# Three gathers in fp32 and a router without GpSimd in a mixture-of-experts layer

## The chip, the cores and the metric

The kernel runs on one core of one Trainium2 chip. Its time is the device time of one execution, in microseconds (us). Before the change it was 1368.84 us, the median of three runs (1368.73, 1368.84, 1371.41).

## The reference, cut to what matters

One transformer-like layer: a token mixer (two recurrent branches), then a mixture-of-experts block of 32 experts with the best four for each of 256 tokens. The change touches the passage from the mixer to the experts and the first visits of the experts.

```python
x = x + g1[:, None, :] * rmsnorm(yl, norm_mix_post[l])
hl = modulate(rmsnorm(x, norm_ffn_pre[l]), sh2, sc2)
# moe_ffn(hl, ...):
logits = xf.astype(f32) @ w_router + b_router
top_v, top_e = lax.top_k(logits, TOP_K)            # 4 of 32
wts = jax.nn.softmax(top_v, axis=-1)
...                                                # tokens sorted by expert, xblk: tokens of expert e
gate, up = jnp.split(xblk @ w_gu[e] + b_gu[e], 2, axis=-1)
gate = jnp.minimum(gate, 7.0); up = jnp.clip(up, -7.0, 7.0)
act = (up + 1) * gate * jax.nn.sigmoid(1.702 * gate)
y = act @ w_dn[e] + b_dn[e]                        # weighted, summed per token
```

D_MODEL and the experts' width are 1024; w_gu of an expert is 1024 x 2048 fp32 (8 MB), w_dn 1024 x 1024 fp32 (4 MB). All 32 experts are read in every run, 403 MB in all.

## The kernel before, in words

**Visits.** The 256 tokens lie as two chunks of 128 on the partitions. Behind the mixer come 33 visits: one for each expert in the list `turn`, and one extra for the fullest expert. A visit serves up to 64 tokens. It gathers them (a product of the normed tokens with a 0/1 matrix `oh`, so the tokens come out transposed, and `modulated` on ScalarE applies scale and shift, L1382), multiplies them with w_gu (`products`, L1600: eight groups k of rows, in the two PSUM banks pg and pu), applies the gate (`gated`, L1610 to L1616), transposes the result (`act_T`, L1629 to L1631), multiplies with w_dn (`down`, L1650), takes the result in two parts (`two_parts`, L1641 and L1642), and adds it to the tokens it came from (`scatter`, L1660, with VectorE's weighted sum into `acc`, which is the space `h2`). The bias goes first into pg and pu (`bias`, L1338).

**Order in a visit.** A visit n begins with the bias, `act_T` of the visit before, the down products of the visit before, then its own gate and up products with the two scatters of the visit before between them, then `gated`. The first two visits have no result to scatter yet; the first visit's down products and scatter stand at the end of visit n = 1.

**Weights.** They come in chunks of 2 MB through a ring of nine buffers. SyncE's queue issues the loads in order; each waits until TensorE has used up the chunk that was in its buffer. Exceptions are the first expert's chunks: its fourth is two halves of 1 MB, one in `scr_`, one in the second half of the tile `xr`, which is `h2`. Then follow the second expert's w_dn, the third's w_gu (four loads) and w_dn (two), the fourth's w_gu, and so on.

**A gather in three parts.** The normed tokens are kept as three bf16 parts, hb0, hb1, hb2, whose sum has fp32's precision: hb0 = bf16(x1 r2), hb1 = bf16(x1 r2 - hb0), hb2 = the rest. A gather is 3 parts x 2 chunks x 8 blocks = 48 products of 128x128 weights with 64 columns of bf16 (L1572; L1376 for the first gather).

**The passage before the visits.** Everything from L1386 on is under a written-out order (`manual_schedule`): each engine runs its instructions in the order of the code. For each chunk: `residual` (VectorE), `squares` (ScalarE), the norm r2 (`second_norm` and its end), transposes (`turned`), logits on TensorE, `logits_back`, `select` (VectorE: best four, 0/1 matrix mbf), the ranks of the tokens within their expert (products with mbf into `rk`), `token_slots` (VectorE: R and the first expert's oh0). Beside it the parts are made: `part(0)` and `part(1)` on ScalarE, `rest` (the remainder, kept in fp32 in h2) on GpSimd for chunk 0 and VectorE for chunk 1, `part(2)` on GpSimd, the last one on VectorE (L1359). Then `first_tokens` (TensorE) for each chunk, `modulated`, and the first visit.

Of the kernel before, what the change touches and what calls it, by code (L numbers as in the profile page):

```python
# [17 lines left out]
P = 128  # L18
# [46 lines left out]
def layer_kernel(ctx: ExitStack, tc, x, ctxt, w_ada, b_ada, n_mix_post, n_ffn_post, w_in, b_in, w_pa, w_pb, w_out,  # L65
# [1038 lines left out]
    for i, u in enumerate(units[1:], 1):  # L1104
        ada_runs[:] = [0] if (i, 0) in rest_at or (i, 1) in rest_at else []
        if u[2]:
            u[2]()
        cur, nxt = nxt, prep(units[i + 1] if i + 1 < len(units) else (lambda: mraw[0],))
        for j, blk in enumerate(u[1](*cur)):
            blk()  # L1110
            for _ in range(rest_at.get((i, j), 0)):
                next(rest)
            if len(convs) > 2 or i > 0 and convs:
                with after(mods[-1:]):
                    convs.pop(0)()
            step(2 if work and len(work) <= 2 or i > 11 else 1)
            for f, *args in load_at.get((i, j), ()):
                if not gu_first:
                    step(100)
                    M["stack"].close()  # L1120
                    vps.close()
                    fps.close()
                    wr1 = pool("wr1", stack=moe)
                    rl = pool("rl", stack=moe)
                    hb0, hb2 = (rl.tile([P, 2, D], BF, name=n) for n in ("hb0", "hb2"))
# [164 lines left out]
    oh0 = hmh[:, 1024:1088].bitcast(BF).rearrange("p (c s) -> p c s", c=2)  # L1290
    hb = [hb0, hb1, hb2]
    big = hmh[:, 1152:1216].rearrange("p (c e) -> p c e", c=2)
    lgs = [None, None]
# [16 lines left out]
    def logits_back(ch, lT):  # L1310
# [2 lines left out]
        lgs[ch] = psm.tile([P, 4, E], F32, name="lgs", tag="tr", bufs=1)  # L1313
        nc.tensor.transpose(lgs[ch].rearrange("p k e -> p (k e)"), l_sb, ident)

    def select(ch):

        nc.vector.tensor_reduce(lsum[:, ch], lgs[ch].rearrange("p k e -> p e k"), AX.X, OP.add)
# [9 lines left out]
    def bias(u, e, n=CAP, sel=None):  # L1328
# [5 lines left out]
        bank = p_.tile([P, 512], F32, name=t, tag=t, bufs=1 + (t == "sc"))[:, 0:W]  # L1334
        sel = pk if sel is None else sel
        for g in range(G):
            j, c0 = divmod(D * u + W * g, 512)
            nc.tensor.matmul(bank[n * g:n * g + n, :], sel[:, 4 * e + j:4 * e + j + 1].to_broadcast([P, n]),  # L1338
                             bgu[:, c0:c0 + W], start=True, stop=False, skip_group_check=True)
        return bank  # L1340

    def biases(*args, **kw):
        return [bias(u, *args, **kw) for u in range(2)]

    def token_slots(ch):

        nc.vector.tensor_scalar(big[:, ch], mbf[:, ch], -BIG, BIG, op0=OP.mult, op1=OP.add)
        nc.vector.tensor_add(R[:, ch], rk[:, ch], big[:, ch])
        nc.vector.tensor_scalar(oh0[:, ch], iot, R[:, ch, turn[0]:turn[0] + 1], None, op0=OP.is_equal)
# [6 lines left out]
    def part(i, ch, hf, eng=nc.scalar):  # L1356
        d, h, x_, r2 = blocks4(hb[i], ch, hf), paired(h2, ch, hf), paired(x1, ch, hf), yss[:, 2 + ch:3 + ch]
        if i == 2:
            eng.tensor_tensor(d, h, blocks4(hb1, ch, hf), op=OP.subtract)  # L1359
        elif i == 1:  # L1360
            nc.scalar.copy(d, h)
        else:
            nc.scalar.activation(d, x_, AF.Identity, scale=r2)

    def rest(ch, hf, eng):
        h, x_, r2, h0 = paired(h2, ch, hf), paired(x1, ch, hf), yss[:, 2 + ch:3 + ch], blocks4(hb0, ch, hf)
        if eng is nc.vector:
            eng.scalar_tensor_tensor(h, x_, r2, h0, op0=OP.mult, op1=OP.subtract)
        else:
            eng.tensor_scalar(h, x_, r2, None, op0=OP.mult)  # L1370
            eng.tensor_tensor(h, h, h0, op=OP.subtract)

    def first_tokens(ch):
        for i in range(3):
            for k in range(KB):
                nc.tensor.matmul(xp[:, k], hb[i][:, ch, k * P:(k + 1) * P], oh0[:, ch],  # L1376
                                 start=(ch == 0 and i == 0 and k == 0), stop=(ch == 1 and i == 2), skip_group_check=True)
# [5 lines left out]

    t00, t01 = turned(0, 0), turned(0, 1)
    end2()
    end1 = leave(1, 1, lambda: first_norm(1))  # L1386
    pmm_.close()
    pb = pool("pb", PSUM, moe)
    nc.scalar.copy(xT[0][0], t00)
    nc.scalar.copy(xT[0][1], t01)  # L1390
    part(0, 0, 0)
    rest(0, 0, nc.gpsimd)
    lT = logits(0)
    end1()
# [22 lines left out]
    part(0, 1, 0)
    part(0, 1, 1)
    part(1, 0, 1)
    part(2, 0, 0, nc.gpsimd)  # L1420
# [12 lines left out]
    oh1 = hmh[:, 1088:1152].bitcast(BF).rearrange("p (c s) -> p c s", c=2)
    for ch in range(2):
        nc.vector.tensor_scalar(oh1[:, ch], iot, R[:, ch, turn[1]:turn[1] + 1], None, op0=OP.is_equal)
    first_tokens(1)
# [293 lines left out]
    visits.insert(HV + 1, (EH, E))  # L1730
    NV = len(visits)
    prev = None
    xgs, ohs, ohTs = {0: xg}, {1: oh1}, {0: ohT}
    for n, (e, col) in enumerate(visits):
        final = n == NV - 1
        if n >= 2 and col < E:
# [24 lines left out]
        if n + 2 < NV and n < 2:  # L1761
            ohs[n + 2] = selection(visits[n + 2][1])
        if n > 1:
            products(banks, gu, xgs[n], range(0, 2))
            scatter(pcol, ohTs[n - 1], 0)
            if n + 2 < NV:
                ohs[n + 2] = selection(visits[n + 2][1])
            products(banks, gu, xgs[n], range(2, 3))
            scatter(pcol, ohTs[n - 1], 1)
            if n < NV - 1:  # L1770
                ohTs[n + 1] = slots(ohs[n + 1])
            products(banks, gu, xgs[n], range(3, KB))
        else:
# [5 lines left out]
            if n == 0:  # L1779
                ohTs[1] = slots(ohs[1])  # L1780
# [93 lines left out]
```

## Time and profile before

| | us |
|---|---|
| median of three runs | 1368.84 |
| lowest, highest | 1368.73, 1371.41 |
| the profiled execution | 1369.44 |
| its span in the trace | 1367.7 |
| busy in the span: TensorE | 1267.9 (93%) |
| VectorE, ScalarE, GpSimd | 562.3, 363.0, 140.9 |
| weight loads and other DMA | 474.14 MB, mean 347 GB/s |

An execution's time is some 2 us above the span of its trace. The passage from the mixer to the experts lies at 404 to 431 us of the span, the first visit at 431 to 450, the second at 450 to 475, the third from 475 on; the visits end at the end of the span. TensorE's clock is given as a share of 2.4 GHz (PEclk). "DMA share" is the mean busy share of the 16 DMA engines. A matmul's record lasts longer than the distance to the next one, since they are pipelined; where a pace is wanted, the starts of rows are compared.

### The profile page before, as it was taken

What the parts mean: (1) busy time and instruction counts of PE and PEld (TensorE: products, weight loads), DVE (VectorE), ACT (ScalarE), POOL (GpSimd) and SP (SyncE); (2) the same over time, 40 slices, a digit from 0 to 9 for tenths busy, and PEclk for the clock granted to TensorE, in tenths of its full rate; (3) what the DMA queues carried; (4) which work ended last, traced back from release to release, by engine and by line L of the source; (5) the groups of instructions that cost most, each with busy time, mean ns of one, the idle gap of its engine ahead of it and who ended that gap; (6) DMA issues with size and microseconds to landing.
All of it is one profiled execution on the core that took longest, in us unless ns stands there. A gap on an engine that the chain in (4) does not pass through costs nothing. (4 is left out here: it accounts for less than half of the span.)

```text
span 1367.7 us, 21197 instructions
## 1 busy us (share of the span) xinstructions
PE 1267.9 (93%) x8827; PEld 642.0 (47%) x8827; DVE 562.3 (41%) x1199; ACT 363.0 (27%) x710; POOL 140.9 (10%) x147
## 2 busy tenths in 40 slices
PE   4998887899997999999999999999999999999995
PEld 2788665699993333333333333333333333333321
DVE  4699477787668222322232223222222222222224
ACT  3557262446645121112111211111111111111102
POOL 4543335300013000000000000000000000000000
PEclk9999999999997999999999999999999999999997
DMA  9732625746887899999999999999999999999994
GB/s 325 245 96 62 215 68 205 255 126 213 308 305 297 358 407 427 427 427 427 426 425 428 426 414 427 427 425 427 426 426 426 428 426 427 426 428 425 427 422 162
DMA packets 78426, 474.14 MB, mean 347 GB/s; under 512 B 6048, under 2 KB 45480, under 8 KB 50672
## 3 DMA queue, kind: packets, MB, share of 16 engines
q1 hardware_dynamic: 77936, 472.54, 85.4%
q8 instruction: 71, 1.16, 0.3%
q14 instruction: 35, 0.29, 0.1%
q0 software_dynamic: 384, 0.15, 0.0%
HBM read 471.60 MB, written 1.07 MB: 346 GB/s over the span
## 5 line engine op out<-in xcount | busy, mean ns | idle before, releaser
L1600 PE MATMUL pg<-wc,hmh 128*64 128x512 f32 x1048 | 273.0, 600 | 14.1 <-DMA wc<-in_w_gu_dram 13.8
L1600 PE MATMUL pu<-wc,hmh 128*64 128x512 f32 x1048 | 269.8, 594 | 0.0
L1650 PE MATMUL dnl<-wc,hmh 128*64 128x512 f32 x1056 | 236.5, 599 | 9.6 <-ACT hmh L1631 9.3
L1650 PEld LDWEIGHTS dnl<-wc,hmh 128*64 128x64 f32 x1056 | 73.6, 137 | 169.5 <-issue 135.6
L1611 ACT ACTIVATE scr<-scr 128x512 f32<-128x512 f32 (+1 forms) x34 | 20.9, 619 | 488.3 <-DVE scr L1610 488.3
L1642 DVE TENSOR_TENSOR ys<-dnl,ys 128x512 fp32r<-128x512 f32 x32 | 22.1, 691 | 310.7 <-ACT ys L1641 310.7
L1600 PEld LDWEIGHTS pu<-wc,hmh 128*64 128x64 f32 x1048 | 74.6, 137 | 151.4 <-issue 151.4
L1600 PEld LDWEIGHTS pg<-wc,hmh 128*64 128x64 f32 x1048 | 67.4, 137 | 146.7 <-issue 110.0
L1666 DVE SCALAR_TENSOR_TENSOR xr<-sc,wv,xr 128x512 f32<-128x512 f32 x124 | 87.3, 746 | 112.6 <-PE sc L1660 112.6
L1610 DVE TENSOR_SCALAR scr<-pg 128x512 f32<-128x512 f32 (+1 forms) x34 | 22.9, 675 | 223.7 <-PE pg L1600 223.7
L237 PE MATMUL mm<-xh,wp 128*128 128x256 f32 (+1 forms) x576 | 107.8, 332 | 4.3 <-DVE hi_sb L511 3.2
L1708 POOL TENSOR_TENSOR scr<-xr,g2n 128x512 f32<-128x512 f32 x2 | 2.5, 1262 | 906.3 <-issue 906.3
L237 PEld LDWEIGHTS mm<-xh,wp 128*128 128x128 f32 x576 | 88.0, 196 | 14.8 <-issue 4.2
L1382 ACT ACTIVATE hmh<-xp,s2c,a2c 128x64 f32<-128x64 f32 x264 | 81.8, 416 | 39.6 <-PE xp L1572 37.5
L1641 ACT CAST ys<-dnl 128x512 fp32r<-128x512 f32 x32 | 18.8, 586 | 232.1 <-PE dnl L1650 232.1
L1572 PEld LDWEIGHTS <-hb 128*128 128x128 bf16 x1024 | 47.5, 99 | 24.5 <-issue 23.5
L228 DVE TENSOR_TENSOR wp<-w,wp 128x2048 fp32r<-128x2048 f32 x21 | 48.6, 2313 | 14.4 <-ACT wp L226 14.4
L237 PE MATMUL mm<-xl,wp 128*128 128x256 f32 (+1 forms) x288 | 53.0, 327 | 0.0
L226 ACT CAST wp<-w 128x2048 fp32r<-128x2048 f32 x25 | 47.5, 1901 | 16.8 <-DMA w<-in_w_in_dram 7.9
L1572 PE MATMUL xp<-oh,hb 128*128 128x64 bf16 x992 | 49.8, 195 | 0.0
L1660 PE MATMUL sc<-ys,ohT 64*128 64x512 f32 x256 | 47.7, 446 | 2.0 <-DVE xr L1664 1.1
L1572 PE MATMUL xp<-oh,ada_sb 128*128 128x64 bf16 x496 | 47.6, 194 | 0.0
(625 smaller groups left out, 1541.9 us busy)
## 6 DMA issues: line engine op xcount, KB each, us to landing
wc<-in_w_gu_dram SPq DMA_DIRECT2D x119, 2048.0 KB, 25.2
wc<-in_w_dn_dram SPq DMA_DIRECT2D x63, 2048.0 KB, 25.7
w<-in_w_in_dram SPq DMA_DIRECT2D x26, 1024.0 KB, 5.6
w<-in_w_ada_dram SPq DMA_DIRECT2D x16, 1024.0 KB, 4.9
wc<-in_w_gu_dram SPq DMA_DIRECT2D x16, 1024.0 KB, 27.1
aw<-in_w_ada_dram SPq DMA_DIRECT2D x8, 1024.0 KB, 11.7
w<-in_w_pa_dram SPq DMA_DIRECT2D x2, 1024.0 KB, 5.6
w<-in_w_out_dram SPq DMA_DIRECT2D x2, 1024.0 KB, 6.4
```

The lines of the kernel that those rows point to most:

```text
L226: nc.scalar.copy(hi, w)
L228: eng.tensor_tensor(lo, w, hi.bitcast(F32), op=OP.subtract)
L237: nc.tensor.matmul(o, ls[k][a], rs[k][b], start=(i + k == 0), stop=(i == 2 and k == n - 1))
L1382: nc.scalar.activation(xg[:, k], xp[:, k], AF.Identity, scale=a2c[:, k:k + 1], bias=s2c[:, k:k + 1])
L1572: nc.tensor.matmul(xp[:, k], part[:, ch, k * P:(k + 1) * P], oh[:, ch], start=(i == 0), stop=(i == 5))
L1600: nc.tensor.matmul(banks[u][n * g:n * g + n, :], xg[:, k], rows_[:, c0:c0 + W], start=False, stop=(k == KB - 1), skip_group_check=True)
L1610: nc.vector.tensor_scalar(g_, cut(banks[0], i), 7.0, None, op0=OP.min)
L1611: nc.scalar.activation(s_, g_, AF.Sigmoid, scale=1.702)
L1642: nc.vector.tensor_sub(ys[1], b, ys[0].bitcast(F32))
L1650: nc.tensor.matmul(b[64 * hf:64 * hf + 64, :], aT_[:, j, g], dn[g][:, j, hf * 512:hf * 512 + 512], start=(g == 0 and j == 0), stop=(g == 1 ...
L1660: nc.tensor.matmul(s[hf], ohT[ps_, ch * P:(ch + 1) * P], ys[i][ps_], start=(i == 0), stop=(i == 1))
L1666: nc.vector.scalar_tensor_tensor(dst, s[hf], wv[:, ch, col:col + 1], dst, op0=OP.mult, op1=OP.add)
```

## The change

The normed tokens are first kept as they are, in fp32 (`hn`, in the space of hb0 and hb2). The first three gathers are made from hn with fp32 0/1 matrices (oh0f, oh1f, oh2f): 2 chunks x 8 blocks = 16 products, two records each. The three bf16 parts are made later: hb0 and chunk 0's other parts at the end of the second visit (n = 1), between the first down products and their scatter; chunk 1's in the third visit (n = 2). GpSimd has nothing to do in the passage. The gathers for the second and third expert stand within visits 0 and 1, the one for the fourth within visit 2. In visit 1 the biases and first products come before `act_T`.

```diff
+                    hn_ = rl.tile([P, 2 * D], F32, name="hn")
+                    hn = hn_.rearrange("p (c d) -> p c d", c=2)
+                    hb0, hb2 = (hn_[:, i * D:(i + 1) * D].bitcast(BF).rearrange("p (c d) -> p c d", c=2) for i in range(2))
...
+    oh0f, oh1f, oh2f = (ada_sb[:, 0, i * P:(i + 1) * P].rearrange("p (c s) -> p c s", c=2) for i in range(3))
...
+    def normed(ch, hf):
+        nc.scalar.activation(hn[:, ch, halves_[hf]], x1[:, ch, halves_[hf]], AF.Identity, scale=yss[:, 2 + ch:3 + ch])
+    def part0(ch, hf):
+        nc.scalar.activation(blocks4(hb0, ch, hf), paired(x1, ch, hf), AF.Identity, scale=yss[:, 2 + ch:3 + ch])
+    def parts12(ch, hf):
+        t = hmh[:, 1536:2048].rearrange("p (j q) -> p j q", j=4)
+        b = blocks4(hb1, ch, hf)
+        nc.vector.scalar_tensor_tensor(t, paired(x1, ch, hf), yss[:, 2 + ch:3 + ch], blocks4(hb0, ch, hf), op0=OP.mult,
+                                       op1=OP.subtract)
+        nc.scalar.copy(b, t)
+        nc.vector.tensor_tensor(blocks4(hb2, ch, hf), t, b, op=OP.subtract)
+    def first_tokens(xp, oh, ch):
+        for k in range(KB):
+            nc.tensor.matmul(xp[:, k], block_of(hn[:, ch], k), oh[:, ch], start=(ch == 0 and k == 0), stop=(ch == 1),
+                             skip_group_check=True)
...
+    def between():
+        nc.scalar.copy(xT[0][0], t00)
+        return first_norm(1)
+    end1 = leave(1, 1, between)
+    nc.vector.tensor_copy(xT[0][1], t01)
     pmm_.close()
     pb = pool("pb", PSUM, moe)
-    nc.scalar.copy(xT[0][0], t00)
-    nc.scalar.copy(xT[0][1], t01)
-    part(0, 0, 0)
-    rest(0, 0, nc.gpsimd)
+    banks = [bias(0, turn[0], sel=ident)]
     lT = logits(0)
+    for hf in range(2):
+        normed(0, hf)
     end1()
     residual(1, 0)
-    squares(1, 0)
     t10 = turned(1, 0)
     logits_back(0, lT)
+    squares(1, 0)
     residual(1, 1)
     squares(1, 1)
     t11 = turned(1, 1)
+    banks.append(bias(1, turn[0], sel=ident, gs=(0,)))
     nc.vector.tensor_copy(xT[1][0], t10)
+    nc.scalar.copy(xT[1][1], t11)
+    router_sum(0)
     end2 = second_norm(1)
-    nc.scalar.copy(xT[1][1], t11)
-    part(0, 0, 1)
-    rest(0, 1, nc.gpsimd)
+    select(0)
     lT = logits(1)
     logits_back(1, lT)
-    select(0)
     end2()
+    for hf in range(2):
+        normed(1, hf)
...
     nc.tensor.matmul(rk[:, 0], tri, mbf[:, 0], start=True, stop=True)
-    banks = biases(turn[0], sel=ident)
+    nc.tensor.matmul(rk[:, 1], onb, mbf[:, 0], start=True, stop=False)
+    token_slots(0)
+    router_sum(1)
     select(1)
-    part(1, 0, 0)
...
-    part(2, 0, 1, nc.gpsimd)
-    token_slots(0)
-    nc.tensor.matmul(rk[:, 1], onb, mbf[:, 0], start=True, stop=False)
+    first_tokens(xp, oh0f, 0)
+    bias(1, turn[0], sel=ident, gs=(1,), bank=banks[1])
     nc.tensor.matmul(rk[:, 1], tri, mbf[:, 1], start=False, stop=True)
-    first_tokens(0)
-    rest(1, 0, nc.vector)
...
-    rest(1, 1, nc.vector)
-    part(1, 1, 1)
     token_slots(1)
-    part(2, 1, 1, nc.vector)
...
+    first_tokens(xp, oh0f, 1)
     xg = hmh[:, 0:512].rearrange("p (k c) -> p k c", k=KB)
     modulated(xg, xp)
...
-        if prev:
+        if n == 1:
+            pcol, pdn, pu = prev
+            ohTs[0] = slots(oh0)
+            banks = biases(e)
+            products(banks, gu, xgs[1], range(0, 2))
+            aT_ = act_T(pu)
+        elif prev:
...
-            if n > 1:
-                two_parts(down(pdn, aT_))
+            two_parts(down(pdn, aT_))
+            if n == 2:
+                parts12(1, 0)
...
         if n > 1:
             products(banks, gu, xgs[n], range(0, 2))
             scatter(pcol, ohTs[n - 1], 0)
             if n + 2 < NV:
                 ohs[n + 2] = selection(visits[n + 2][1])
+            if n == 2:
+                parts12(1, 1)
             products(banks, gu, xgs[n], range(2, 3))
             scatter(pcol, ohTs[n - 1], 1)
...
-            products(banks, gu, xgs[n], range(3, KB))
+            if n == 2:
+                products(banks, gu, xgs[n], range(3, 6))
+                xgs[3] = gather(ohs[3], at=3)
+                products(banks, gu, xgs[n], range(6, KB))
+            else:
+                products(banks, gu, xgs[n], range(3, KB))
         else:
-            products(banks, gu, xgs[n], range(0, 4))
-            if n == 0:
-                xgs[1] = gather(ohs[1], at=1)
+            products(banks, gu, xgs[n], range(2 * n, 4))
+            if n == 1:
+                nc.vector.tensor_copy(oh2f, ohs[2])
+            xp = px.tile([P, KB, CAP], F32, name="xp", tag="xp")
+            for ch in range(2):
+                first_tokens(xp, (oh1f, oh2f)[n], ch)
+            xgs[n + 1] = hm4[(n + 1) % 2].rearrange("p (k c) -> p k c", k=KB)
+            modulated(xgs[n + 1], xp)
+            if n == 1:
+                ohTs[1] = slots(oh1)
             products(banks, gu, xgs[n], range(4, KB))
...
         u = gated(banks, last=final)
         if n == 1:
             two_parts(down(pdn, aT_))
             for ch in range(2):
+                part0(ch, 0)
+                part0(ch, 1)
+                parts12(0, ch)
                 scatter(pcol, ohTs[0], ch, True)
...
-        if n + 2 < NV:
+        if 1 < n < NV - 2:
             xgs[n + 2] = gather(ohs[n + 2], at=n + 2)
```

## Rows read from the trace of the kernel before

**Rows 1.** windows of all engines; PE, PEld, DVE, ACT, POOL busy, PEclk, DMA share, GB/s

```profile
415.00:435.00 20.00, 14.65 (x97) 6.72 (x99) 17.78 (x55) 11.74 (x21) 9.51 (x6) 0.50 0.70 288
...
425.00:440.00 15.00, 11.69 (x73) 4.70 (x70) 13.03 (x50) 5.17 (x12) 3.23 (x2) 0.66 0.40 137
...
450.00:460.00 10.00, 8.68 (x49) 3.23 (x46) 2.10 (x5) 4.63 (x11) 0.00 (x0) 1.00 0.52 184
...
460.00:485.00 25.00, 23.03 (x144) 9.29 (x142) 6.60 (x10) 4.18 (x11) 0.00 (x0) 0.93 1.01 429
...
485.00:495.00 10.00, 10.00 (x50) 3.25 (x48) 0.69 (x1) 0.59 (x1) 0.00 (x0) 1.00 0.92 368
...
495.00:1300.00 805.00, 784.36 (x4898) 281.54 (x4898) 204.15 (x353) 121.35 (x319) 0.00 (x0) 1.00 1.01 426
```

**Rows 2.** page, costliest groups: count, busy us, mean ns, idle before and its releaser

```profile
L1600 PE MATMUL pg<-wc,hmh 128*64 128x512 f32 x1048 | 273.0, 600 | 14.1 <-DMA wc<-in_w_gu_dram 13.8
```

**Rows 3.** timeline of SyncE's DMA queue: start, duration, line, load, count

```profile
410.07 5.77 SPq L1077 DMA_DIRECT2D wc<-in_w_dn_dram  x2
...
429.96 0.33 SPq L1726 DMA_DIRECT2D xr<-in_w_gu_dram  x1
...
436.71 3.76 SPq L1077 DMA_DIRECT2D wc<-in_w_dn_dram  x2
...
445.23 19.77 SPq L1067 DMA_DIRECT2D wc<-in_w_gu_dram  x4
...
468.10 3.76 SPq L1077 DMA_DIRECT2D wc<-in_w_dn_dram  x2
...
474.96 20.84 SPq L1067 DMA_DIRECT2D wc<-in_w_gu_dram  x4
```

**Rows 4.** timeline of TensorE, 410 to 485 us: start, duration, idle before in brackets

```profile
412.50 0.91 PE L1306 MATMUL lT<-hmh,wr_sb 128*32 128x128 f32 x16 [1.90 <-ACT hmh L1389]
...
430.91 1.97 PE L1600 MATMUL pg<-wc,hmh 128*64 128x512 f32 x4
...
440.03 0.20 PE L1572 MATMUL xp<-hmh,hb 128*128 128x64 bf16 x1
...
441.41 0.19 PE L1572 MATMUL xp<-hmh,hb 128*128 128x64 bf16 x1
...
448.45 0.28 PE L1586 MATMUL op__4698<-idb,hmh 128*64 128x128 bf16 x4
...
453.25 1.08 PE L1338 MATMUL pu<-bgu,pk 128*64 128x512 f32 x4
...
454.15 1.03 PE L1600 MATMUL pg<-wc,hmh 128*64 128x512 f32 x4
...
467.89 7.04 PE L1650 MATMUL dnl<-wc,hmh 128*64 128x512 f32 x32
...
484.94 7.05 PE L1650 MATMUL dnl<-wc,hmh 128*64 128x512 f32 x32
```

**Rows 5.** timeline of VectorE, 419 to 430 us

```profile
419.85 1.31 DVE L271 TENSOR_TENSOR nwt<-nwt,nwt 128x1 f32<-128x1 f32 x1
...
421.27 0.28 DVE L1318 TENSOR_REDUCE ada_sb<-lgs 128x32 f32<-128x128 f32 x1
...
423.22 0.17 DVE L1347 TENSOR_SCALAR hmh<-mbf 128x32 f32<-128x32 bf16 x1
...
423.90 3.28 DVE L1368 SCALAR_TENSOR_TENSOR xr<-xr,yss,hb 128x512 f32<-128x512 f32 x2
...
428.84 1.06 DVE L1359 TENSOR_TENSOR hb<-xr,ada_sb 128x512 bf16<-128x512 f32 x1
```

**Rows 6.** timeline of ScalarE, 409 to 424 us

```profile
409.67 0.60 ACT L1231 ACTIVATE xr<-mm 128x512 f32<-128x512 f32 x1 [0.38 <-PE mm L1226]
...
421.39 2.31 ACT L1363 ACTIVATE hb<-xr,yss 128x512 bf16<-128x512 f32 x2 [2.19 <-DVE yss L272]
```

**Rows 7.** one line's instructions, L874: duration min, median, max in ns; first and last start

```profile
L874 PE MATMUL sbp<-wr_sb,s2c x16: 246/276/276, 285.8 to 287.4; 128*128 128x32 f32 x16
```

More of the change, by code (lines that the diff above doesn't have):

```diff
@@ L1124, in layer_kernel @@
                     rl = pool("rl", stack=moe)
-                    hb0, hb2 = (rl.tile([P, 2, D], BF, name=n) for n in ("hb0", "hb2"))
+                    hn_ = rl.tile([P, 2 * D], F32, name="hn")
+                    hn = hn_.rearrange("p (c d) -> p c d", c=2)
+                    hb0, hb2 = (hn_[:, i * D:(i + 1) * D].bitcast(BF).rearrange("p (c d) -> p c d", c=2) for i in range(2))
                 f(*args)
@@ L1289, in layer_kernel @@
     eq = hmh[:, 1792:2048].rearrange("p (c j e) -> p c j e", c=2, j=4)
-    oh0 = hmh[:, 1024:1088].bitcast(BF).rearrange("p (c s) -> p c s", c=2)
+    oh0, oh1 = (a.bitcast(BF).rearrange("p (c s) -> p c s", c=2) for a in (hmh[:, 1024:1088], ada_sb[:, 0, 384:448]))
+    oh0f, oh1f, oh2f = (ada_sb[:, 0, i * P:(i + 1) * P].rearrange("p (c s) -> p c s", c=2) for i in range(3))
     hb = [hb0, hb1, hb2]
@@ L1314, in logits_back, with router_sum @@
         nc.tensor.transpose(lgs[ch].rearrange("p k e -> p (k e)"), l_sb, ident)
+    def router_sum(ch):
+        nc.vector.tensor_reduce(lsum[:, ch], lgs[ch].rearrange("p k e -> p e k"), AX.X, OP.add)
     def select(ch):
-        nc.vector.tensor_reduce(lsum[:, ch], lgs[ch].rearrange("p k e -> p e k"), AX.X, OP.add)
         nc.vector.scalar_tensor_tensor(lg[:, ch], lsum[:, ch], yss[:, 2 + ch:3 + ch], br_sb, op0=OP.mult, op1=OP.add)
@@ L1326, in select, with bias @@
             nc.vector.tensor_reduce(mbf[:, ch], eq[:, ch].rearrange("p j e -> p e j"), AX.X, OP.add)
-    def bias(u, e, n=CAP, sel=None):
+    def bias(u, e, n=CAP, sel=None, gs=None, bank=None):
         G = P // n
@@ L1333, in bias @@
         p_, t = (((pb, "pg"), (pb, "pu")) if n == CAP else ((pb, "dn"), (pm, "sc")))[u]
-        bank = p_.tile([P, 512], F32, name=t, tag=t, bufs=1 + (t == "sc"))[:, 0:W]
+        if bank is None:
+            bank = p_.tile([P, 512], F32, name=t, tag=t, bufs=1 + (t == "sc"))[:, 0:W]
         sel = pk if sel is None else sel
-        for g in range(G):
+        for g in range(G) if gs is None else gs:
             j, c0 = divmod(D * u + W * g, 512)
@@ L1348, in token_slots @@
         nc.vector.tensor_add(R[:, ch], rk[:, ch], big[:, ch])
-        nc.vector.tensor_scalar(oh0[:, ch], iot, R[:, ch, turn[0]:turn[0] + 1], None, op0=OP.is_equal)
+        nc.vector.tensor_scalar(oh0f[:, ch], iot, R[:, ch, turn[0]:turn[0] + 1], None, op0=OP.is_equal)
     paired = lambda a, ch, hf: a[:, ch, halves_[hf]].rearrange("p (q j) -> p j q", j=4)
     blocks4 = lambda a, ch, hf: a[:, ch, halves_[hf]].rearrange("p (j q) -> p j q", j=4)
[L1356 to L1377, printed above, removed]
+    def normed(ch, hf):
+        nc.scalar.activation(hn[:, ch, halves_[hf]], x1[:, ch, halves_[hf]], AF.Identity, scale=yss[:, 2 + ch:3 + ch])
@@ L1385, in layer_kernel @@
     end2()
-    end1 = leave(1, 1, lambda: first_norm(1))
+    def between():
[3 more added lines that the diff above has]
+    nc.vector.tensor_copy(xT[0][1], t01)
     pmm_.close()
     pb = pool("pb", PSUM, moe)
-    nc.scalar.copy(xT[0][0], t00)
-    nc.scalar.copy(xT[0][1], t01)
-    part(0, 0, 0)
-    rest(0, 0, nc.gpsimd)
+    banks = [bias(0, turn[0], sel=ident)]
     lT = logits(0)
+    for hf in range(2):
+        normed(0, hf)
     end1()
     residual(1, 0)
-    squares(1, 0)
     t10 = turned(1, 0)
     logits_back(0, lT)
+    squares(1, 0)
     residual(1, 1)
@@ L1413, in layer_kernel @@
     nc.tensor.matmul(rk[:, 0], tri, mbf[:, 0], start=True, stop=True)
-    banks = biases(turn[0], sel=ident)
+    nc.tensor.matmul(rk[:, 1], onb, mbf[:, 0], start=True, stop=False)
+    token_slots(0)
+    router_sum(1)
     select(1)
-    part(1, 0, 0)
[L1417 to L1420, printed above, removed]
-    part(2, 0, 1, nc.gpsimd)
-    token_slots(0)
-    nc.tensor.matmul(rk[:, 1], onb, mbf[:, 0], start=True, stop=False)
-    nc.tensor.matmul(rk[:, 1], tri, mbf[:, 1], start=False, stop=True)
-    first_tokens(0)
-    rest(1, 0, nc.vector)
-    part(1, 1, 0)
-    part(2, 1, 0, nc.gpsimd)
-    rest(1, 1, nc.vector)
-    part(1, 1, 1)
-    token_slots(1)
-    part(2, 1, 1, nc.vector)
[L1433 to L1436, printed above, removed]
+    first_tokens(xp, oh0f, 0)
+    bias(1, turn[0], sel=ident, gs=(1,), bank=banks[1])
+    nc.tensor.matmul(rk[:, 1], tri, mbf[:, 1], start=False, stop=True)
+    for ch in range(2):
+        nc.tensor.matmul(rk[:, 2], onb, mbf[:, ch], start=(ch == 0), stop=(ch == 1))
+    token_slots(1)
+    first_tokens(xp, oh0f, 1)
     xg = hmh[:, 0:512].rearrange("p (k c) -> p k c", k=KB)
@@ L1439, in layer_kernel @@
     for ch in range(2):
-        nc.tensor.matmul(rk[:, 2], onb, mbf[:, ch], start=(ch == 0), stop=(ch == 1))
+        nc.vector.tensor_scalar(oh1f[:, ch], iot, R[:, ch, turn[1]:turn[1] + 1], None, op0=OP.is_equal)
     nc.vector.tensor_copy(big[:, 0], rk[:, 2])
@@ L1515, in layer_kernel @@
     exchanged(wv, wsel)
+    for oh, ohf in ((oh0, oh0f), (oh1, oh1f)):
+        nc.vector.tensor_copy(oh, ohf)
     show("R", R.rearrange("p a b -> p (a b)"))
@@ L1714, in count @@
         return nc.values_load(src, engines=engines, min_val=0, max_val=T + CAP)
-    ohT = slots(oh0)
     gu_first.append([scr_, xr[:, 2 * D:4 * D]])
@@ L1732, in layer_kernel @@
     prev = None
-    xgs, ohs, ohTs = {0: xg}, {1: oh1}, {0: ohT}
+    xgs, ohs, ohTs = {0: xg}, {}, {}
     for n, (e, col) in enumerate(visits):
@@ L1758, in layer_kernel @@
                 sum_bias(n % 2, bias_mm(n % 2, pm.tile([P, 512], F32, name="b", tag="sc", bufs=2)))
-            if n > 1:
-                two_parts(down(pdn, aT_))
-        if n + 2 < NV and n < 2:
+            two_parts(down(pdn, aT_))
+            if n == 2:
+                parts12(1, 0)
+        if n < 2:
             ohs[n + 2] = selection(visits[n + 2][1])
@@ L1771, in layer_kernel @@
                 ohTs[n + 1] = slots(ohs[n + 1])
-            products(banks, gu, xgs[n], range(3, KB))
-        else:
-            products(banks, gu, xgs[n], range(0, 4))
-            if n == 0:
-                xgs[1] = gather(ohs[1], at=1)
+            if n == 2:
[4 more added lines that the diff above has]
+                products(banks, gu, xgs[n], range(3, KB))
+        else:
+            products(banks, gu, xgs[n], range(2 * n, 4))
+            if n == 1:
+                nc.vector.tensor_copy(oh2f, ohs[2])
+            xp = px.tile([P, KB, CAP], F32, name="xp", tag="xp")
+            for ch in range(2):
+                first_tokens(xp, (oh1f, oh2f)[n], ch)
[3 more added lines that the diff above has]
+                ohTs[1] = slots(oh1)
             products(banks, gu, xgs[n], range(4, KB))
-            if n == 0:
-                ohTs[1] = slots(ohs[1])
         u = gated(banks, last=final)
```

## The prediction

> **What bounds the kernel now.** I read the stages first. From 495 to 1300 us the 16 DMA engines are busy all the time (share 1.01, 426 GB/s) [rows 1]; a 2 MB load takes 2.097/427, about 4.9 us. TensorE is busy beside them, and the line of the gate and up products shows who is late in the end: of its idle time, 13.8 us waits for a w_gu load [rows 2]. So the weight stream sets the end. Once it is unbroken, TensorE may come later by up to that 13.8 us at no cost; what counts is how long the stream stands still before. The same windows say where: 0.60 x 15 = 9.0 us in 425 to 440, 0.48 x 10 = 4.8 in 450 to 460, 0.08 x 10 = 0.8 in 485 to 495, 14.6 us in all [rows 1]. The change lies in that stretch, so its worth is the change of this sum, one to one.
>
> Then SyncE's queue tells why the stream stands [rows 3]. It is in order. The last load of the first expert (xr, 1 MB, into the space of h2) goes at 429.96, 14.1 us behind the w_dn pair, when VectorE's last pass over h2 has ended (428.84 + 1.06 [rows 5]); two loads of the second expert's w_dn follow at 436.71 and 440.1, when the first visit has used up the chunks of products 0-1 and 2-3; the four of the third expert's w_gu start at 445.23 (after products 4-5), and three more follow as the second visit frees products 0-1, 2-3, 4-5; then at 468.10 two w_dn (products 6-7; first half of the down products), at 474.96 the fourth expert's w_gu (second half of them), whose second chunk needs half of the next down products, 484.94 + 3.5 [rows 4].
>
> **What the change does to that sequence.** Call S the start of the first visit's products, 430.91 before [rows 4].
>
> *The xr load.* h2 is now written last by ScalarE's square at 409.67 [rows 6] and read by nothing, so the load stands only behind the w_dn pair in SyncE's queue, which is out at 415.84 [rows 3]. I read the stream as dry at about 426 before; with 1 MB (2.45 us) more it is dry at 428.5.
>
> *The front.* Removed: all GpSimd passes, ScalarE's eight strided passes (four first parts, 421.39: 1.15 each [rows 6], and four casts), VectorE's two rests and its last part (428.84: 1.06 [rows 5]). Gone with GpSimd are long small operations such as 419.85, 1.31 us for one column, where 32 columns take 0.17 at 423.22 [rows 5]. New are four ScalarE passes into hn, which lie beside VectorE's chain. That chain is now alone on the path: the second chunk's norm needs its squares at about 415.3 as before (the second w_dn, which waits for them, goes at 415.84 [rows 3]); two norm operations, then the first selection, 1.65 without its reduction (the undisturbed one with it runs 421.27 to 423.22, 1.95 [rows 5]), to 417.3; three norm operations, 417.9; the order (423.22 to 423.90 [rows 5], 0.7), 418.6; the second selection, 420.7. TensorE starts the first chunk's tokens at 418.75.
>
> *An fp32 gather.* A product is two records here. The nearest row has 128x128 fp32 weights and 32 columns: 16 records start within 1.6 us, 107 ns each [rows 7]. Bounds: 33 ns, as the 48 bf16 records of a gather in 1.57 us (440.03 to 441.60 [rows 4]), and 215 ns, the same row at the half clock. I take 107: 3.4 us for the 32 records, 1.9 more than now, and twice that at 1.2 GHz. In this stretch the granted clock is 0.50 now [rows 1], that is 1.2 GHz, after a front in which TensorE has mostly waited; the change shortens those waits but does not remove them, so I take half clock for the front: 3.4 us per chunk. First chunk done 422.2, half a bias 423.1, the rank products and the order 423.9, second chunk 427.3, the first modulated block 0.5. If the clock is back halfway through, 426. I take S = 427.0, and 4.5 us for products 0-1 (5.8 now at half clock, 3.45 at full: 16 groups from 454.15 to 467.89 are 0.86 each [rows 4]).
>
> [...]
>
> *The first two visits.* The second gather now stands between products 3 and 4 (3.4 us instead of 1.57); the one for the third expert leaves the gap after the first visit's products (their end is the slots' start, 448.45 [rows 4]), where it hid beside VectorE, and enters the second visit (3.4, with the slots 3.7). In its place the two biases and products 0-1 no longer wait for the gated values: 1.25 us, an estimate, for VectorE to begin and read the first bank, 2 x 0.90 for the biases (453.25 to 454.15 [rows 4]). So, with S = 427.0: w_dn loads may go at 431.5 and 435.0; w_gu of the third expert at 435.0 + 3.4 + 3.45 = 441.9; products end 445.3; 1.25 + 1.8 + 3.45: 451.8; transposes 0.75: 456.0; gather, slots: 463.2; then 466.6; down 7.0 [rows 4]: 470.1 and 473.6.
>
> *Between the two down products.* Now 467.89 + 7.04 to 484.94, 10.0 us [rows 4], with a gather of 1.6 us at full clock in it. After, the gather is gone, but ScalarE has four first parts (1.15 each) and two contiguous casts (0.6, as 409.67 [rows 6]) ahead of the copy that act_T needs, VectorE two differences from 1.06 (428.84) to 1.64 (423.90 [rows 5]) and two of at most 1.06 ahead of the scatter's evacuations, and TensorE stands about 3 us before the second scatter, which should bring the half clock for the biases. With the lower price: act_T's copy ends at 9.5, at half clock 10.4 and the second bias at 10.7 to 12. I take 11.3, so the chunk is free 14.8 behind 473.6, at 488.4. In the third visit the two other parts hold the second scatter for about 1 us; products run behind it, and the stream has a backlog by then: nothing. The gather of the fourth expert, moved ahead of products 6-7, waits for VectorE's last part, done 11 us after the down products, before its turn; its DVE and ACT work is hidden. GpSimd's queue keeps what it has in the visits; SyncE's order of loads is unchanged.
>
> **The sum.** Data flows 1.2 us after an issue (429.96 and the window behind it). Before, by this bookkeeping: dry 426.0 to 431.2, 5.2; 433.7 to 437.9, 4.2; three loads to 452.6, dry to 458.8, 6.2; six loads to 488.3, dry to 489.6, 1.3: 16.9 (14.6 by the windows, since a load's edges are blurred). After: 428.5 to 432.7, 4.2; two loads to 442.5, dry to 443.1, 0.6; one to 448.0, dry to 453.0, 5.0; two to 462.8, dry to 464.4, 1.6; four to 484.0, dry to 489.6, 5.6: 17.0. What the front gives, the two fp32 gathers and the pause in the third visit take back: +0.1 us on the profiled execution's 1369.44, which is 0.6 above the median of the runs shown (1368.84). Forecast 1369.0. Its own error is S, 2 us to each side.
>
> **Rivals.** *The clock holds in the front* (27%). The bias products and logits now close TensorE's gap of 1.90 us ahead of 412.50 [rows 4], and if 2.4 GHz is granted through 415 to 427, both chunks take 1.7 and S is 424.5. Then 0.9, 0.6, 5.0, 1.5 and 5.6: 13.6 us dry, 3.4 less, 1365.6. Against it: TensorE still stands in several gaps from 415 to 419.
> *The fp32 gather costs by columns* (5%). The 512-column records are 0.86 us for four, so 64 columns in 32 records are 1.7 us. S is 424.0, each of the next two gathers 1.7 us less: 10.3 dry, 1362.3. Against it: rows 7.
> *The pause before the third visit decides* (23%, slower). Place: ScalarE's and VectorE's parts between the first and second down products. If the differences take 1.64, ScalarE's copy waits for both, and TensorE goes into the down products at the half clock, those start at 13 and their first half takes 5 instead of 3.5: the chunk comes 3.2 us later, and every us behind my 11.3 is a us of the end: 1372.2. For it: the clock of 0.93 in 460 to 485 [rows 1], after a shorter pause of the same kind.
> *The xr load is held still* (in the 45% of the forecast): if anything keeps it behind 427, up to 2.5 us return.
>
> **The numbers.** What can be told from no change is 0.2%, 2.7 us. Forecast 45%: 5 faster, 36 same, 4 slower. Clock holds 27%: 23 faster, 4 same. Columns 5%: faster. Pause 23%: 20 slower, 3 same. Together faster 33%, same 43%, slower 24%. The likeliest case's own range is 1366.5 to 1371.5; for 8 in 10 it reaches to both neighbours, 1363.5 to 1373.5.
>
> **What will show it.** Right: xr issued near 416; fp32 records at about 107 or 214 ns; first products at 427; the dry stretches near 429, 449 and 485. Wrong: a stream that is not dry behind 440, first products before 424, or TensorE waiting for w_gu before 1000 us.

## The result and the profile after

The changed kernel takes 1386.51 us, the median of four runs (1383.94 to 1387.34); the kernel before took 1368.78 beside it (1367.39 to 1371.41). The ratio is 1.0124, interval 1.0103 to 1.0145: 17.7 us slower. Forecast were 1369.0 and a range up to 1373.5. The profiled execution after took 1387.34 us, its span is 1385.5.

First the gathers, which the prediction priced at 107 ns a record. One line's instructions after, columns as in [rows 7]:

```profile
L1380 PEld LDWEIGHTS xp<-ada_sb,hn x96: 307/330/333, 417.9 to 473.2; 128*128 128x128 f32 x96
L1380 PE MATMUL xp<-ada_sb,hn x96: 397/437/464, 417.9 to 473.3; 128*128 128x64 f32 x96
```

TensorE's timeline after, the places that answer to [rows 4]:

```profile
417.92 4.00 PE L1380 MATMUL xp<-ada_sb,hn 128*128 128x64 f32 x16 [0.92 <-DVE ada_sb L1356]
...
424.68 3.96 PE L1380 MATMUL xp<-ada_sb,hn 128*128 128x64 f32 x16 [0.66 <-DVE ada_sb L1356]
429.14 1.98 PE L1601 MATMUL pg<-wc,hmh 128*64 128x512 f32 x4 [0.50 <-ACT hmh L1386]
...
435.58 1.02 PE L1601 MATMUL pg<-wc,hmh 128*64 128x512 f32 x4
...
439.11 7.72 PE L1380 MATMUL xp<-ada_sb,hn 128*128 128x64 f32 x32
446.76 1.98 PE L1601 MATMUL pg<-wc,hmh 128*64 128x512 f32 x4
...
452.93 1.02 PE L1601 MATMUL pg<-scr,hmh 128*64 128x512 f32 x4
...
466.03 7.73 PE L1380 MATMUL xp<-ada_sb,hn 128*128 128x64 f32 x32
...
473.90 1.92 PE L1601 MATMUL pg<-wc,hmh 128*64 128x512 f32 x4
...
481.86 7.03 PE L1651 MATMUL dnl<-wc,hmh 128*64 128x512 f32 x32
...
493.88 1.87 PE L1661 MATMUL sc<-ys,ohT 64*128 64x512 f32 x4 [3.07 <-DVE xr L1665]
...
500.28 7.03 PE L1651 MATMUL dnl<-wc,hmh 128*64 128x512 f32 x32
```

By the starts, 32 records take 446.76 - 439.11 = 7.65 us, 239 ns each. The 16 at 417.92 and the 16 at 424.68 take the same (4.00 and 3.96), though the mean granted clock is 0.95 over the first and 0.50 over the second: this pace does not follow the clock. What follows does: four-record groups start 1.7 us apart until 434 and again from 446.76, where 0.86 is the full-clock pace of [rows 4]. By the groups' 2048 columns that is 2.4 columns per ns at clock 1.00 and 1.2 at 0.50, an estimate from the distances of 0.86 and 1.7 us; the prediction's 2.4 and 1.2 GHz are these two clocks. The clock falls within the second gather, from 1.00 to 0.50, as windows of one us show (columns as in [rows 1]: PE, PEld, DVE, ACT, POOL busy, PEclk, DMA share, GB/s):

```profile
441.00:442.00 1.00, 1.00 (x6) 1.00 (x6) 0.00 (x0) 0.00 (x0) 0.00 (x0) 0.97 0.92 393
442.00:443.00 1.00, 1.00 (x6) 1.00 (x5) 0.00 (x0) 0.00 (x0) 0.00 (x0) 0.50 0.92 393
```

SyncE's DMA queue after, the loads of [rows 3]:

```profile
409.97 4.89 SPq L1077 DMA_DIRECT2D wc<-in_w_dn_dram  x2
414.91 0.42 SPq L1726 DMA_DIRECT2D xr<-in_w_gu_dram  x1
435.79 3.76 SPq L1077 DMA_DIRECT2D wc<-in_w_dn_dram  x2
453.14 25.83 SPq L1067 DMA_DIRECT2D wc<-in_w_gu_dram  x4
482.07 3.76 SPq L1077 DMA_DIRECT2D wc<-in_w_dn_dram  x2
488.94 22.19 SPq L1067 DMA_DIRECT2D wc<-in_w_gu_dram  x4
```

The xr load goes 15 us earlier, at 414.91 as forecast (416), and the two w_dn loads behind it 0.9 earlier. Every load behind those goes later: the third expert's w_gu at 453.14 instead of 445.23, the fourth's at 488.94 instead of 474.96. The windows after show what that does to the stream (columns as above):

```profile
425.00:440.00 15.00, 14.50 (x52) 7.18 (x51) 9.35 (x50) 2.96 (x10) 0.00 (x0) 0.66 0.43 159
440.00:460.00 20.00, 20.00 (x84) 10.87 (x85) 3.55 (x8) 4.39 (x10) 2.37 (x5) 0.74 0.66 268
460.00:480.00 20.00, 20.00 (x90) 11.69 (x88) 0.42 (x1) 3.08 (x9) 0.00 (x0) 0.83 0.59 223
480.00:500.00 20.00, 16.00 (x66) 5.48 (x64) 9.96 (x14) 7.45 (x9) 0.00 (x0) 0.83 0.96 410
500.00:510.00 10.00, 10.00 (x48) 3.23 (x46) 1.75 (x2) 0.77 (x2) 0.00 (x0) 1.00 0.53 200
510.00:1300.00 790.00, 768.41 (x4826) 276.29 (x4822) 201.99 (x350) 120.75 (x318) 0.00 (x0) 1.00 1.00 425
```

The stream is dry for 0.57 x 15 = 8.6, 0.34 x 20 = 6.8, 0.41 x 20 = 8.2, 0.8 and 0.47 x 10 = 4.7 us: about 29, where [rows 1] had 14.6. Over one window for both kernels, 410 to 515, the dry time is 28.4 after and 13.7 before. That is 14.7 of the 17.8 us by which the spans differ. Some 2 us more lie in the unbroken stretch from 515 on (425 GB/s instead of 426 over 815 us). Most of that is a few stretches of 10 us: 810 to 820 and 830 to 840 go at 360 and 362 GB/s after, while the slowest before, 790 to 800 and 800 to 810, go at 405 and 401. Why is not known. And the end is still the stream's, as the page's costliest group says, which answers to [rows 2]:

```profile
L1601 PE MATMUL pg<-wc,hmh 128*64 128x512 f32 x1048 | 276.2, 607 | 16.0 <-DMA wc<-in_w_gu_dram 15.4
```

### The profile page after: what moved, and what is told of

Same layout as the page of the kernel before. It is cut to its first block, busy times and chain, and to the rows that moved or that the text cites. A ratio compares the mean times of both kernels' runs of the same rounds, so it can differ in the third digit from the quotient of the medians.

```text
span 1385.5 us, 21101 instructions
## 1 busy us (share of the span) xinstructions
PE 1287.9 (93%) x8779; PEld 659.1 (48%) x8779; DVE 560.3 (40%) x1208; ACT 364.0 (26%) x713; POOL 130.1 (9%) x140
## 5 line engine op out<-in xcount | busy, mean ns | idle before, releaser
L1601 PE MATMUL pg<-wc,hmh 128*64 128x512 f32 x1048 | 276.2, 607 | 16.0 <-DMA wc<-in_w_gu_dram 15.4
L1573 PEld LDWEIGHTS <-hn 128*128 128x128 bf16 x960 | 43.7, 98 | 24.3 <-issue 24.3
L1573 PE MATMUL xp<-oh,hn 128*128 128x64 bf16 x960 | 47.2, 193 | 0.0
L237 PEld LDWEIGHTS mm<-xl,wp 128*128 128x128 f32 x288 | 44.4, 196 | 4.2
```

Source lines behind the costliest of these rows:

```text
L237: nc.tensor.matmul(o, ls[k][a], rs[k][b], start=(i + k == 0), stop=(i == 2 and k == n - 1))
L1573: nc.tensor.matmul(xp[:, k], part[:, ch, k * P:(k + 1) * P], oh[:, ch], start=(i == 0), stop=(i == 5))
L1601: nc.tensor.matmul(banks[u][n * g:n * g + n, :], xg[:, k], rows_[:, c0:c0 + W], start=False, stop=(k == KB - 1), skip_group_check=True)
```

## The experiments

Two things were open: whether the record's price comes from the *step* with which the weights are read (block_of takes every fourth column of hn, so neighbouring weights lie 16 bytes apart), and what else in the two visits sets the dry time. Each run is compared with the kernel before, run on the same chip (medians 1368.46 for the first four, 1367.99 for the rest); the first four and the rest ran on two chips, so between them the ratios are the safer comparison.

### Weights without a step

The normed tokens are written in block order, so that a block's 128 columns lie together; all else is the changed kernel.

```diff
-        nc.scalar.activation(hn[:, ch, halves_[hf]], x1[:, ch, halves_[hf]], AF.Identity, ...)
+        nc.scalar.activation(blocks4(hn, ch, hf), paired(x1, ch, hf), AF.Identity, ...)
...
-            nc.tensor.matmul(xp[:, k], block_of(hn[:, ch], k), oh[:, ch], ...)
+            nc.tensor.matmul(xp[:, k], hn[:, ch, k * P:(k + 1) * P], oh[:, ch], ...)
```

> The changed kernel with hn written in block order, so that the weights of a fp32 gather lie in adjacent columns instead of every fourth; ScalarE's four passes into hn read with a step instead. Theory STEP (the step of the weights makes a record 0.24 us): records of L1380 fall from 0.24 to about 0.11 us at 2.4 GHz, a gather from 7.7 to 3.5 to 4 us, the half clock behind the second gather (442 to 452) goes or shortens, the stream's dry time falls from 29 to 15 to 18 us, and the time from 1386.5 to 1371 to 1375. Theory FP32 (any fp32 product of 128x128 weights with 64 columns costs 0.24): records stay at 0.24, time 1384 to 1388. Theory CLOCK (the records are slow because the clock is): records stay above 0.2 wherever PEclk is 0.5 and are 0.11 elsewhere in both kernels.

Measured: 1368.98 us, median of 12 runs (1364.06 to 1375.84), ratio to before 0.9996, interval 0.9986 to 1.0007. The whole loss is gone; expected were 1371 to 1375. The profiled execution is its longest run (1375.84), so its places, not its end, are read. TensorE's timeline of this kernel:

```profile
419.26 3.39 PE L1380 MATMUL xp<-ada_sb,hn 128*128 128x64 f32 x16 [0.92 <-DVE ada_sb L1356]
...
438.39 3.79 PE L1380 MATMUL xp<-ada_sb,hn 128*128 128x64 f32 x32
442.11 1.08 PE L1601 MATMUL pg<-wc,hmh 128*64 128x512 f32 x4
...
458.69 3.79 PE L1380 MATMUL xp<-ada_sb,hn 128*128 128x64 f32 x32
...
469.41 7.03 PE L1651 MATMUL dnl<-wc,hmh 128*64 128x512 f32 x32
...
488.01 7.03 PE L1651 MATMUL dnl<-wc,hmh 128*64 128x512 f32 x32
```

A gather takes 3.72 us, 116 ns a record, about half; contiguous records do follow the clock (3.39 for 16 in the front at 0.55, and 2.00 at 1.00 in later runs). And the groups behind the second and third gather go at full clock. So one edit takes away both parts of the loss. Dry time in 410 to 515 is 14.7 us even in this longest run, near before's 13.7.

### The step by itself

A kernel that computes no layer: series of 32 products with 128x128 weights from one tile (64 records in fp32, 32 in bf16 and for transposes), between full-size products. It ran once. One series, and how its weights are taken:

```diff
+    def every(step, a, i):
+        return a[:, i % 2, 0:P * step:step]
...
+        for i in range(N):
+            nc.tensor.matmul(xp[:, 0:64], every(4, xs, i), oh[:, 0:64], start=True, stop=True)
+        warm()
...
```

> No layer is computed: series of 32 products each by themselves, a warm-up of 512 columns between them, weights 128x128, one operand taken with a step. Theory STEP: fp32, 64 columns: about 0.107 us a record at step 1, about 0.24 at step 4 and at step 8, between them or 0.11 at step 2; 0.24 also with 256 columns at step 4 (the weights bound it), bf16 at step 4 dearer than 0.033 or not (open), columns with a step of 4 at most 0.12. Theory FP32: 0.24 at every step.

TensorE's timeline of this kernel; L108, L111, L114, L117 are steps 1, 2, 4 and 8, L120 is step 4 with 256 columns, L123 and L126 are bf16 with step 4 and 1, L129 has the step in the columns, L132 and L135 are transposes of a block with step 1 and 4:

```profile
26.26 7.25 PE L108 MATMUL xp<-oh,xs 128*128 128x64 f32 x64
...
41.99 7.64 PE L111 MATMUL xp<-oh,xs 128*128 128x64 f32 x64
...
58.10 14.97 PE L114 MATMUL xp<-oh,xs 128*128 128x64 f32 x64
...
83.28 15.27 PE L117 MATMUL xp<-oh,xs 128*128 128x64 f32 x64
...
109.67 15.08 PE L120 MATMUL xp<-oh,xs 128*128 128x256 f32 x64
...
133.16 1.23 PE L123 MATMUL xp<-ob,xb 128*128 128x64 bf16 x32
...
142.90 1.10 PE L126 MATMUL xp<-ob,xb 128*128 128x64 bf16 x32
...
152.50 7.56 PE L129 MATMUL xp<-oh,xs 128*128 128x64 f32 x64
...
168.48 3.66 PE L132 MATMUL tr<-ident,xs 128*128 128x128 f32 x32
...
180.56 4.00 PE L135 MATMUL tr<-ident,xs 128*128 128x128 f32 x32
```

By the distance of starts, an fp32 record costs 111 ns at step 1, 117 at 2, 231 at 4, 235 at 8. Four times the columns change nothing (233), so here the weights set the pace. bf16 at step 4 takes 33 ns against 29. So step 2 of fp32 and step 4 of bf16 are nearly free, and steps 4 and 8 of fp32 cost double, both nearly the same. The transposes don't follow: with step 4 of fp32 the distance rises there only from 109 to 120 ns. So that the step makes a product's record slow is shown; why it does, and why it hardly touches a transpose, is not.

The clock of the series, in windows of the same kernel (PE, PEld, DVE, POOL busy, PEclk, DMA share, GB/s):

```profile
42.00:49.00 7.00, 7.00 (x62) 7.00 (x60) 0.00 (x0) 0.00 (x0) 1.00 0.00 0
...
58.00:73.00 15.00, 15.00 (x66) 14.89 (x65) 0.00 (x0) 0.00 (x0) 0.66 0.00 0
...
83.30:98.00 14.70, 14.70 (x64) 14.70 (x62) 0.00 (x0) 0.00 (x0) 0.61 0.00 1
...
109.70:124.50 14.80, 14.80 (x65) 14.80 (x64) 0.00 (x0) 0.00 (x0) 1.00 0.00 0
```

All four are without a gap in TensorE's records. The clock falls in the series of steps 4 and 8 with 64 columns (means 0.66 and 0.61) and stays at 1.00 with the same slow weights and 256 columns. It also stays at 1.00 in the series of step 2 with 64 columns, which lasts as long (7.64 us) as a slow gather. So in these rows slow weights with 64 columns come ahead of the fall, as in the second gather of the changed kernel, and what follows starts at the lower clock: there groups 1.7 us apart for 0.86, here 10.42 and 11.32 us for the 20 full-size products behind steps 4 and 8, 8.64 behind step 1.

### The pause before the third visit

The two parts (part0, parts12) of chunk 0 go ahead of the down products' evacuation, beside the down products; weights keep their step.

```diff
-            two_parts(down(pdn, aT_))
+            b = down(pdn, aT_)
             for ch in range(2):
                 part0(ch, 0)
                 part0(ch, 1)
                 parts12(0, ch)
+            two_parts(b)
+            for ch in range(2):
                 scatter(pcol, ohTs[0], ch, True)
```

> The changed kernel, but the parts made at the end of the second visit stand ahead of the down product's two parts in ScalarE's and VectorE's order, beside the down products instead of behind them. Weights still every fourth column. Theory PAUSE (what lies between the first and second down products is paid one to one): the distance from the end of the first down products to the start of the second falls from 11.4 to 6 to 8 us, the dry 4.8 us of the stream at 500 to 510 go by as much, time 1381 to 1383. Theory BACKLOG (the stream has enough queued loads there): the distance falls, the time stays within 1 us of 1386.5.

Measured: 1384.67 us (1380.58 to 1386.31, 5 runs), ratio 1.0103, interval 1.0087 to 1.0119. The starts of the two down products lie 17.77 us apart instead of 18.42. That is a fraction of what was expected: the evacuation now stands behind the parts, TensorE waits 1.87 us for it instead of 0.69, and the two biases still run at 0.5 (1.92 and 1.98). Beside after, the intervals overlap; alone it decides nothing.

The same edit upon the first experiment's kernel:

> Both edits together. Theories STEP and PAUSE: the two savings add, since both are dry time of one stream: dry time 10 to 13 us, time 1366 to 1370, that is no slower than the kernel before. If only STEP holds 1371 to 1375, if only PAUSE 1381 to 1383, if neither 1386.

Measured: 1364.41 us (1363.05 to 1366.16, 5 runs), ratio 0.9967, interval 0.9954 to 0.9980; 4.6 us less than without it and below the 1366 to 1370 expected. Two lines of its TensorE timeline:

```profile
416.29 2.00 PE L1380 MATMUL xp<-ada_sb,hn 128*128 128x64 f32 x16 [0.91 <-DVE ada_sb L1356]
...
477.58 7.03 PE L1651 MATMUL dnl<-wc,hmh 128*64 128x512 f32 x32
```

The down products start at 462.28 and 477.58, 15.30 apart against 18.60. Dry time in 410 to 515 is 7.4 us instead of 14.7, but only about half of that is the edit's. Up to 462 both kernels have the same code; in this execution the first gather ran at clock 1.00, in the first experiment's at 0.55, and from its start to the first down products it is 46.0 us here and 50.2 there. In 480 to 500, behind the edit, dry time goes from 5.2 us (DMA share 0.74) to 1.8 (0.91), 3.4 less beside 3.3 of distance. So the pause is paid about one to one here. Why the same edit gives so little on the changed kernel is open: in that execution ScalarE's two pairs of part0 took 3.51 and 2.98 us, here 2.37 each.

### Four edits upon that kernel

*act_T first.* The second visit's order of before: its first products wait for the gated values again.

```diff
-            banks = biases(e)
-            products(banks, gu, xgs[1], range(0, 2))
+            banks = [bias(0, e)]
             aT_ = act_T(pu)
+            banks.append(bias(1, e))
+            products(banks, gu, xgs[1], range(0, 2))
```

> Base is e3_both, 1364.4. The second visit in the old order: bias, transposes of the first visit's result, bias, then products 0-1, so that TensorE waits for the gated values again. Theory ORDER (the change's reordering is worth the wait it avoids): products 0-1 of the second visit end some 2 us later, and so does all behind them: 1366 to 1367. Rival SLACK: the stream has loads queued there, nothing moves: 1364 to 1365.

Measured: 1366.32 us (1362.52 to 1374.97, 12 runs), ratio 0.9986, interval 0.9971 to 1.0002: 1.9 more by the medians, with intervals that overlap. The size fits, but is not proved.

*The first visit's scatter later.* The scatter moves into the third visit: chunk 0 ahead of that visit's down products, chunk 1 and the slots behind them.

```diff
-            two_parts(down(pdn, aT_))
+            if n == 2:
+                scatter(visits[0][1], ohTs[0], 0, True)
+            b = down(pdn, aT_)
+            if n == 2:
+                scatter(visits[0][1], ohTs[0], 1, True)
+                ohTs[2] = slots(ohs[2])
+            two_parts(b)
...                            # and the scatter and the slots go from the end of n == 1
```

> Base e3_both. The first visit's scatter stands behind the third visit's biases and transposes, its second chunk behind the second down products, so that TensorE doesn't stand between the two down products for VectorE's weighted sums. Theory PAUSE: the distance between the down products falls from 8.3 to 3.5 to 5 us, the last dry time of the stream (480 to 485) goes, time 1360 to 1362. Rival BACKLOG: 1364 to 1365.

Measured: 1361.70 us (1358.80 to 1363.75, 6 runs), ratio 0.9946, interval 0.9929 to 0.9962. It beats the kernel before and the changed one; beside 1364.41 it is 2.7 less, as expected, with intervals that just overlap. TensorE's timeline of this one:

```profile
463.54 7.03 PE L1651 MATMUL dnl<-wc,hmh 128*64 128x512 f32 x32
470.41 1.02 PE L1345 MATMUL pg<-bgu,pk 128*64 128x512 f32 x4
471.37 0.75 PE L1630 MATMUL tpa<-ident,scr 128*128 128x128 f32 x4
472.05 1.08 PE L1345 MATMUL pu<-bgu,pk 128*64 128x512 f32 x4
473.06 0.73 PE L1661 MATMUL sc<-ys,ohT 64*128 64x512 f32 x4
473.72 7.09 PE L1651 MATMUL dnl<-wc,hmh 128*64 128x512 f32 x32
```

No idle time stands in brackets any more and the biases take 1.02 and 1.08, full clock: 10.18 us from one down to the next.

*The xr load held.* A one-column copy that reads h2 after the first gather keeps the load until 424.17 (413.51 without it).

```diff
     modulated(xg, xp)
+    nc.scalar.copy(trT[:, 0:1], h2[:, 1, D - 1:D])
```

> Base e3_both. A one-column copy that reads h2 behind the first modulation holds the xr load back from 413.5 to about 425 us. Theory XR (the early load is worth its 2.45 us of stream): 1366 to 1367.5. Rival LAST (the dry time is set by the last load for which the stream waits, the fourth expert's second w_gu chunk, and bytes moved earlier only move the gap): within 0.7 us of 1364.4.

Measured: 1363.91 us (1362.92 to 1371.61, 12 runs), ratio 0.9982, interval 0.9966 to 0.9998. By the medians nothing is lost beside 1364.41, and the two profiled executions have the same dry time (7.4 us in 410 to 515) and spans of 1361.9 and 1362.5. But four of the twelve runs took 1368.1 to 1371.6 us, and the ratios lie 2 us apart with intervals that overlap, so a loss of up to the 2.45 us that XR forecast is not excluded. In the profiled executions the early xr load, the change's clearest move in SyncE's queue, is worth nothing by itself.

*The second gather behind the first visit's products.* The third expert's w_gu goes 4.2 us earlier (434.46 instead of 438.67), the fourth's at the same place (468.94, 469.36).

```diff
-            products(banks, gu, xgs[n], range(2 * n, 4))
+            products(banks, gu, xgs[n], range(2 * n, 4 if n else KB))
...
-            products(banks, gu, xgs[n], range(4, KB))
+                products(banks, gu, xgs[n], range(4, KB))
```

> Base e3_both. The second gather stands behind all products of the first visit instead of between 3 and 4, where it covers the wait for the first bank. Theory EACH (every gap of the stream counts by itself): the third expert's first w_gu load goes 3.8 us earlier, the gap at 445 to 450 shrinks by 2 to 3 us: 1361 to 1362.5. Theory LAST: only the covered wait counts, about 1.2 us: 1363 to 1364.

Measured: 1363.69 us (1362.44 to 1369.07, 9 runs), ratio 0.9968, interval 0.9953 to 0.9982. Again nothing beyond 0.7 us, and the same dry time (7.4). These two runs agree on one reading: the dry time is set by when the *last* load is issued for which the stream still has to wait, the fourth w_gu's second chunk, which the second down products free. The traces bear it out more sharply than the medians: from the start of those down products to the end of the span there are 885.2 us in the changed kernel and 884.8 to 886.0 in six of the experiments, whose spans run from 1361.9 to 1384.0 (882.8 before, where the unbroken stretch is some 2 us shorter). Only *The first visit's scatter later* lies outside, with 887.3; there the stream is no longer dry behind 480 (share 1.01 in 480 to 500), so an earlier load is the last that it waits for.

## Why the prediction was wrong

**The step that failed** is the price of a record, "I take 107: 3.4 us for the 32 records". It measured 239 ns, and 7.65 us for a gather. [Rows 7] was the nearest row in shape and type, but not in layout: its weights are one column repeated, without a step. The bound above, 215, was put down to the half clock and is below the measured value too. The first experiment shows the cause: the same 32 records without the step take 3.72 us, and the kernel takes 1368.98 us. That this is the forecast's 1369.0 almost to the digit is luck: its twelve runs spread over 12 us.

The hint stood in the trace of before. Two lines that transpose 128x128 fp32 blocks, the first from contiguous columns, the second by block_of (weight loads: duration min, median, max in ns):

```profile
L969 PEld LDWEIGHTS tra<-ident,hmh x16: 137/140/143, 349.5 to 354.3; 128*128 128x128 f32 x16
...
L1298 PEld LDWEIGHTS trr<-ident,xr x16: 196/210/230, 409.4 to 415.6; 128*128 128x128 f32 x16
```

The weight load is half as long again with the step, 210 ns for 140. The probe has the same pair (L132, L135), where the distance of starts rises only from 109 to 120 ns, so the price of a product could not have been read from it, but that the layout has one could.

**How it reached the end.** The last load that the stream waits for, the fourth w_gu's second chunk, was forecast to be free at 488.4; by the same rule it was at 500.28 + 3.5 = 503.8, 15.4 later. By the starts in the timeline, against the prediction's terms: S +2.1 (429.14 for 427.0); products 0-1 +1.9 (6.4 for 4.5, half clock); second gather +4.2; the half clock behind it +2.7 (446.76 to 452.93 is 6.2, not 3.45); third gather with its slots +4.2; the half clock behind that +1.1; the biases ahead of products 0-1 -1.2, since no wait for the bank shows; the distance of the down products +0.1. These make 15.1; the rest is rounding of edges. Of it, 8.4 is the price of the records in the second and third gather, and 3.8 the half clock behind those two, which the prediction had nowhere. Another 4.0 lie in S and products 0-1: the first two gathers took 3.9 and 4.0 instead of 3.4 each, and the clock came back at 435, later than was taken.

**What held.** The stream bounds the end, and a change in its dry time is a change of the end: +14.7 of +17.8. The xr load's place; the order of the loads; the first tokens at 417.9 (418.75); the distance of the down products, 18.4 (18.3); dry stretches near 430, 450, 478 and 502 for 429, 449 and 485, the later ones moved by the gathers. TensorE's stand of about 3 us before the second scatter, with the half clock for the biases behind it, came as forecast (3.07; 1.92 us for the first bias). But the bookkeeping that valued each gap led the attention to the xr load, which by the medians is worth nothing (*The xr load held*), instead of to the chain up to the last starved load.

**The rivals.** *Clock holds in the front*: it held through nearly all of the first gather (until 421.5), and that gave nothing, as the records with the step don't follow it (4.00 and 3.96 us for 16 at 0.95 and 0.50). With contiguous weights the same code ran its first gather at 0.55 in one execution (the first experiment's, 3.39 us for 16 records) and at 1.00 in the later ones (2.00): the front's clock differs from execution to execution. *Columns*: refuted, 64 and 256 columns take 14.97 and 15.08 with step 4. Its 1.7 us does not follow from the row that it names, since four records of 512 columns in 0.86 us give 0.86 us for 32 of 64; the probe's full-size products (L99, 20 records in 8.64 us) would give it. A gather took neither: 3.72 us without the step, 7.65 with it. *The pause* gave the right sign for a wrong reason: it came out as in the forecast. The range was at fault by its own rule as well: the bound of 215 ns was named, yet its price, 3.5 us for each of two gathers and more behind, was not carried into it.

## What to carry to other kernels

Take a product's price from a row with the same layout of the weights, not only the same shape and type: here fp32 weights read every fourth column cost a product's record 231 ns for 111 (a transpose's 120 for 109), and writing the tile in block order once took the whole loss away (1368.98 us for 1386.51). Where an in-order stream of loads sets the end, follow the chain to the last load that finds it dry; gaps ahead of that one had no price of their own in these traces. And here the slower pass over few columns was paid twice, once itself (8.4 us) and once in the clock of what followed (3.8).

## What the runs showed of the hardware

- Products with fp32 weights of 128x128: 111, 117, 231, 235 ns a record at steps 1, 2, 4, 8; bf16 29 and 33 at steps 1 and 4; fp32 transposes 109 and 120 at steps 1 and 4.
- The slow records (step 4) do not follow the granted clock: 16 take 4.00 us at 0.95 and 3.96 at 0.50. The contiguous ones do: 2.00 at 1.00, 3.39 at 0.55.
- A step of 4 in the 64 columns, with contiguous weights, costs next to nothing (7.56 for 7.25); since the weights set that pace, it says little of the columns.
- TensorE's clock fell (means 0.66 and 0.61) in two series without any gap in their records, of slow weights with 64 columns, and stayed at 1.00 in the one with 256 columns.
